# Gates of a hybrid block in pairs by seven half-size products, their weights split by accumulating DMA

## The chip, the cores and the metric

One core of a Trainium2 chip runs the kernel. The metric is the device time of one execution in microseconds; the kernel before is told by the median of three runs.

## The reference

One transformer block on 512 tokens of 1024 features, all in fp32. A normed input goes through one wide projection, four branches (attention, spatial gating, a short convolution, a multi-scale pool) give 256 features each, and each branch is widened to 1024 and gated:

```python
h = rmsnorm(x, norm_mix_pre[l])
(..., gate_pre) = split_cols(h @ w_in[l])
gates = jax.nn.sigmoid(gate_pre + gate_b[l]).reshape(B_, S_, N_BRANCH, D_)
...
merged = (gates[:, :, 0] * y_a + gates[:, :, 1] * y_b
          + gates[:, :, 2] * y_c + gates[:, :, 3] * y_d)
x = x + rmsnorm(merged @ w_out[l], norm_mix_post[l])
h = rmsnorm(x, norm_ffn_pre[l])
f = jnp.square(jax.nn.relu(h @ w_ff1[l])) @ w_ff2[l]
x = x + rmsnorm(f, norm_ffn_post[l])
```

`gate_pre` is 512 tokens by 4 x 1024: as a product, 32 output blocks of 128 features by 512 tokens, each over 1024 inputs.

## The kernel before, in words

Each fp32 product is three products of a shorter format. A matrix is held as a high part (a cast) and a low part (matrix minus cast), and `mm3` issues high x high, high x low and low x high. So every weight has to be split: `load` (line 110) has SP fetch 512 KB into one of three `raw` buffers; `split_w` (line 115) casts on ACT (`wh`) and subtracts on DVE (`wl`); `split_by_dma` (line 122) casts on ACT, writes the negated high part by ACT and lets a DMA issued by POOL add the weights from memory to it. Before, only the four early blocks of `w1` are split the second way. `wh` and `wl` have five buffers each, PSUM has eight banks.

**Order.** PE issues in the order of the program text. ACT, DVE, POOL and SP issue each in an order that a scheduler sets when the kernel is built; a waiting instruction holds back all that stands behind it on its engine. All instructions of PE and ACT are issued by a helper and are recorded at line 95, so they are told apart by tile.

**Gate stage.** `z` is the normed input, `zh` and `zl` its two parts, features on partitions, 512 tokens on columns. For each of eight blocks of 128 output features the loop at line 683 calls `gate(b, i)` for the four branches: 24 matmuls of 512 columns into a bank `fb` (line 329), then a product with the row scales `rbc` (line 452). `merge(b)` (line 457) takes sigmoids of the four gates, widens the branches by 24 matmuls with `wB[b]` into banks `y`, multiplies (line 468), adds (line 470), and splits the merged block into `mh` and `ml`. The gates of block 0 stand between the steps of the attention.

**Then** the product with `wO` (`wo`), a norm, and the feed-forward layer. `ff1` (line 718) gives the first four blocks of the hidden layer (`EARLY`, line 761) into banks `z`, first for 256 tokens, then for the other 256. The other blocks of `w1` go in pairs by seven half-size products (line 855): with the weights of a pair cut into four quarters and the input into four, sums of quarters are formed (`raw` combined by DVE; `hsum` of the input), and seven products `pa`, `pb`, `pc`, `pa` again, `pd`, `pc` again, `pa` again of 12 matmuls on 256 columns replace eight. `second()` (line 807) does one block of the second layer, `w2`, into the banks `acc`, with `uh` and `ul`, the two parts of the hidden block.

Of the kernel before, what the change touches and what calls it, by code (L numbers as in the profile page):

```python
# [80 lines left out]
def build(ctx, tc, d, out):  # L81
# [22 lines left out]
    def f(t):  # L104
        return t.bitcast(F32)
# [36 lines left out]
    def sl(pair, *ix):  # L142
        return pair[0][ix], pair[1][ix]
# [305 lines left out]
    def gate(b, i):  # L449
        ps = feature_block("wG", 4 * b + i)  # L450
        g = gp.tile([P, S], F32, tag="g", name="g", bufs=6)
        DVE.tensor_tensor(g, ps, rbc, ALU.mult)  # L452
        return g

    gates = []

    def merge(b):
        for i, g in enumerate(gates):
            ACT.activation(g, g, AF.Sigmoid, bias=k1("gateb")[:, i * 8 + b:i * 8 + b + 1])
        w = weights(d["wB"][b])  # L460
        prev = None
        for i, br in ((1, bT), (2, cT), (3, dT), (0, aT)):
            g = gates[i]
# [12 lines left out]
    others = branches()  # L476

# [188 lines left out]
    right = dict(side="right")  # L666

    TOP = 20
    xp = ctx.enter_context(tc.tile_pool(name="xp", bufs=1, reuse_waits="tile", **right))
    x1 = xp.tile([P, NT, D], F32, name="x1")  # L670
    r2 = xp.tile([P, TOP], F32, name="r2")[:, :NT]
    mp = ctx.enter_context(ExitStack())
    mpool = mp.enter_context(tc.tile_pool(name="mp", bufs=1, reuse_waits="tile", **right))
    mh = mpool.tile([P, KD, S], F32R, name="mh")
    ml = mpool.tile([P, KD, S], F32R, name="ml")
    mT = (mh, ml)
    gmix = mpool.tile([P, D], F32, name="gmix")
    gffn = mpool.tile([P, D], F32, name="gffn")
    for b in range(KD):
        while len(gates) < 4:  # L680
            gates.append(gate(b, len(gates)))
        merge(b)
    nc.sync.dma_start(gmix, d["gmix"].partition_broadcast(P))
    nc.sync.dma_start(gffn, d["gffn"].partition_broadcast(P))
    for t in range(NT):
        nc.sync.dma_start(x1[:, t, :], d["x"][t * P:(t + 1) * P, :])
    s1.close()

    HK, HS = KD // 2, S // 2
    hs = ExitStack()
    hp_ = hs.enter_context(tc.tile_pool(name="hp", bufs=1, reuse_waits="tile"))

# [4 lines left out]
    hsum = [hp_.tile([P, 3, HK, HS], F32R, name=f"hs{c}") for c in "hl"]  # L704
    ws = ExitStack()
    wk_ = ws.enter_context(tc.tile_pool(name="wk", bufs=1, reuse_waits="tile"))
    yg = wk_.tile([P, NT, D], F32, name="yg")
    stt = wk_.tile([P, NT, 4], F32, name="stt")

# [31 lines left out]
    for hf in range(2):  # L741
        wo = [weights(d["wO"][hf, c]) for c in range(4)]
        for t in range(NT):
            ps = bank("wo")
            for k in range(KD):
                mm3(ps, sl(mT, slice(None), k, slice(t * P, (t + 1) * P)),
                    sl(wo[k // 2], slice(None), slice((k % 2) * 512, (k % 2 + 1) * 512)), k == 0, k == KD - 1)
            cols = slice(hf * 512, (hf + 1) * 512)
            sq = wk_.tile([P, D], F32, tag="sq", name="sq", bufs=1)
            ACT.activation(sq[:, :512], ps, AF.Square, accum_out=stt[:, t, hf:hf + 1])  # L750
            DVE.tensor_tensor(yg[:, t, cols], ps, gmix[:, cols], ALU.mult)
            if hf == 0:
# [35 lines left out]
    sst = up.tile([P, 64], F32, name="sst")[:, :4 * NT].rearrange("p (t c) -> p t c", c=4)  # L788
# [50 lines left out]
    A11, A12, A22, S4 = (sl(h2, slice(None), k, t) for k, t in  # L839
                         ((slice(0, HK), slice(0, HS)), (slice(HK, KD), slice(0, HS)), (slice(HK, KD), slice(HS, S)),  # L840
                          (slice(0, HK), slice(HS, S))))
    S1, S2, S3 = (sl(hsum, slice(None), c) for c in range(3))
    fx = hs.enter_context(tc.tile_pool(name="fx", bufs=1, reuse_waits="tile"))
    B1, B2 = slice(0, 512), slice(512, 1024)

    def small():
        return fx.tile([P, HS], F32, tag="x", name="x", bufs=5)

    def part(ps, w, at, a, first):

        for k in range(HK):
            mm3(ps[:, :HS], sl(w, slice(None), slice(at + k * P, at + (k + 1) * P)), sl(a, slice(None), k),
                first and k == 0, k == HK - 1, not first)

    for j in range(EARLY, NFF, 2):
        g, h = u[j], u[j + 1]
        left, rght = load(d["w1"][j]), load(d["w1"][j + 1])
        w = split_w(left)
        w22 = split_w(rght[:, B2], 512)

        DVE.tensor_tensor(left[:, B1], rght[:, B1], left[:, B1], ALU.subtract)
        DVE.tensor_tensor(rght[:, B1], rght[:, B2], rght[:, B1], ALU.subtract)
        DVE.tensor_tensor(rght[:, B2], rght[:, B2], left[:, B1], ALU.subtract)
        DVE.tensor_tensor(left[:, B2], left[:, B2], rght[:, B2], ALU.subtract)
        wl = split_w(left)
        wr = split_w(rght)
        pa, pb = bank("pa"), bank("pb")
        part(pa, w, 0, A11, True)
        x1_ = small()
        ACT.copy(x1_, pa[:, :HS])  # L870
        part(pb, w, 512, A12, True)
        DVE.tensor_tensor(g[:, :HS], pb[:, :HS], x1_, ALU.add)
        if j == EARLY:
            second()
        pc = bank("pc")
        part(pc, wl, 0, S1, True)
        x5 = small()
        ACT.copy(x5, pc[:, :HS])
        part(pa, wr, 512, S2, False)
        x2 = small()  # L880
        ACT.copy(x2, pa[:, :HS])
        pd = bank("pd")
        part(pd, wl, 512, A22, True)
        second()
        part(pc, w22, 0, S4, False)
        DVE.tensor_tensor(h[:, :HS], pc[:, :HS], x2, ALU.add)
        part(pa, wr, 0, S3, False)
        x3 = small()
        ACT.copy(x3, pa[:, :HS])
        DVE.tensor_tensor(g[:, HS:], pd[:, :HS], x3, ALU.add)  # L890
        DVE.tensor_tensor(h[:, HS:], x3, x5, ALU.add)
# [131 lines left out]
```

## Time and profile before

| what | us |
|---|---|
| median of 3 runs (743.75 to 744.67) | 744.11 |
| the profiled execution | 744.92 |
| its span in the trace | 743.2 |
| PE busy | 728.5 |
| DVE busy | 467.2 |
| ACT busy | 356.5 |
| POOL busy | 15.9 |

The profiled execution's own time is its span and what lies around it. Busy times of engines overlap; a matmul's record is longer than the distance to the next (0.39 us against 0.227 for 512 columns), so the time of a group of matmuls is read from the chain, where consecutive ones are joined. Idle time of an engine counts only where another waits for it. The mean granted TensorE clock over the span is 1.00 of its upper level of 2.4 GHz.

### The profile page before, as it was taken

Reading aid. Unit: us, or ns where it says so; the run is one execution under the profiler, and the core shown is the slowest. Engines: PE = TensorE matmul, PEld = TensorE weight load, DVE = VectorE, ACT = ScalarE, POOL = GpSimd, SP = SyncE. Lnnn points to the kernel's source line nnn. Section 1 sums busy time; section 2 is a strip of 40 time slices with the busy share of each in tenths; the row PEclk is TensorE's granted clock in tenths of the full one; section 3 lists DMA queues with packets and bytes.
Section 4 is the critical chain, followed back from the end, with each engine's and each line's share of the span. In section 5 each row is a group of like instructions: output and inputs, shape, how many; then the busy total and the mean of one; then the engine's idle time right before and its main releaser. Section 6 shows DMA issues by size and latency. Waiting matters only on the chain.

```text
span 743.2 us, 10315 instructions
## 1 busy us (share of the span) xinstructions
PE 728.5 (98%) x4058; PEld 636.4 (86%) x4058; DVE 467.2 (63%) x760; ACT 356.5 (48%) x584; POOL 15.9 (2%) x32
## 2 busy tenths in 40 slices
PE   8999999999999999999997999999999999999996
PEld 8998788888888888888887899999999999888885
DVE  7599986355456365365355976777677676774424
ACT  6875444523323232332346756546665556753411
POOL 1110000000000000000011000000000000000001
PEclk9999999999999999999999999999999999999999
DMA  8523222362232322323137033322433233533103
GB/s 304 183 107 114 86 95 73 117 219 94 90 109 86 112 86 90 109 86 111 44 101 198 1 108 120 101 99 86 130 97 114 86 101 127 170 113 112 60 0 114
DMA packets 23728, 80.87 MB, mean 109 GB/s; under 512 B 3072, under 2 KB 3584, under 8 KB 23680
## 3 DMA queue, kind: packets, MB, share of 16 engines
q1 hardware_dynamic: 23072, 78.12, 31.2%
q0 software_dynamic: 608, 2.10, 1.6%
q8 instruction: 32, 0.52, 0.3%
q14 instruction: 16, 0.13, 0.1%
HBM read 78.11 MB, written 2.10 MB: 108 GB/s over the span
## 4 chain that ended last, share of the span: by engine, by line
PE 88%; DVE 5%; DMA 2%; ACT 2%; issue 1%; SPq 0%; POOL 0%; DVEq 0%; ACTq 0%; POOLq 0%
PE fb L95 28%; PE acc L95 23%; PE pa L95 8%; PE y L95 6%; PE wo L95 5%; PE pc L95 5%; PE pd L95 3%; PE pb L95 2%; PE psA L95 2%; PE sgv L95 2%; DMA xT<-in_xT 1%; PE po L95 1%; DMA wl<-in_w 1%; DMA raw<-in_wF 1%; DVE wl L119 1%
## 5 line engine op out<-in xcount | busy, mean ns | idle before, releaser
L95 ACT CAST wh<-raw 128x1024 fp32r<-128x1024 f32 (+2 forms) x154 | 153.7, 1009 | 222.3 <-issue 105.4
L119 DVE TENSOR_TENSOR wl<-raw,wh 128x1024 fp32r<-128x1024 f32 (+2 forms) x150 | 173.8, 1167 | 28.8 <-ACT wh L95 26.5
L95 PE MATMUL fb<-zh,wh 128*128 128x512 f32 x336 | 131.4, 391 | 0.1
L95 PE MATMUL fb<-zl,wh 128*128 128x512 f32 x336 | 130.8, 389 | 0.0
L95 PE MATMUL fb<-zh,wl 128*128 128x512 f32 x336 | 130.8, 389 | 0.0
L95 PE MATMUL acc<-wh,ul 128*128 128x512 f32 x232 | 90.5, 390 | 1.2 <-DVE ul L798 1.2
L95 PE MATMUL acc<-wh,uh 128*128 128x512 f32 x232 | 90.7, 391 | 0.0
L95 PE MATMUL acc<-wl,uh 128*128 128x512 f32 x232 | 90.6, 391 | 0.0
L452 DVE TENSOR_TENSOR g<-fb,rbc 128x512 f32<-128x512 f32 x32 | 22.1, 692 | 96.7 <-PE fb L95 96.7
L798 DVE TENSOR_TENSOR ul<-u,uh 128x512 fp32r<-128x512 f32 x58 | 38.7, 689 | 57.2 <-ACT uh L95 57.1
L95 PEld LDWEIGHTS fb<-zh,wl 128*128 128x128 f32 x336 | 63.1, 188 | 13.2
L95 PEld LDWEIGHTS fb<-zh,wh 128*128 128x128 f32 x336 | 63.1, 188 | 13.2 <-DVE zc L361 0.4
L95 PEld LDWEIGHTS fb<-zl,wh 128*128 128x128 f32 x336 | 63.1, 188 | 12.8
L95 PEld LDWEIGHTS acc<-wh,ul 128*128 128x128 f32 x232 | 43.6, 188 | 11.4 <-DVE ul L798 2.1
L95 PEld LDWEIGHTS acc<-wh,uh 128*128 128x128 f32 x232 | 43.6, 188 | 8.5 <-ACT uh L95 0.4
L95 ACT CAST uh<-u 128x512 fp32r<-128x512 f32 x58 | 34.3, 618 | 34.2 <-PE acc L95 33.7
L95 PEld LDWEIGHTS acc<-wl,uh 128*128 128x128 f32 x232 | 43.6, 188 | 7.9
L95 ACT ACTIVATE u<-u 128x512 f32<-128x512 f32 x60 | 33.2, 622 | 16.3 <-DVE u L890 16.3
L95 PE MATMUL pa<-hsh,wh 128*128 128x256 f32 x112 | 31.3, 280 | 0.5 <-ACT x L95 0.5
L95 PE MATMUL pa<-hsl,wh 128*128 128x256 f32 x112 | 31.2, 279 | 0.0
L95 PE MATMUL pa<-hsh,wl 128*128 128x256 f32 x112 | 31.2, 279 | 0.0
L95 PE MATMUL wo<-wh,mh 128*128 128x512 f32 x64 | 25.1, 392 | 0.0
(313 smaller groups left out, 1419.7 us busy)
## 6 DMA issues: line engine op xcount, KB each, us to landing
raw<-in_w SPq DMA_DIRECT2D x64, 512.0 KB, 3.5
raw<-in_wG SPq DMA_DIRECT2D x32, 512.0 KB, 3.4
raw<-in_wF SPq DMA_DIRECT2D x10, 512.0 KB, 4.1
raw<-in_wB SPq DMA_DIRECT2D x8, 512.0 KB, 3.4
raw<-in_wO SPq DMA_DIRECT2D x8, 512.0 KB, 3.4
xk<-in_x SPq DMA_DIRECT2D x4, 512.0 KB, 9.3
x<-in_x SPq DMA_DIRECT2D x4, 512.0 KB, 5.8
wl<-in_w POOLq DMA_DIRECT2D x4, 512.0 KB, 6.5
```

The lines of the kernel that those rows point to most:

```text
L95: ins = op(*a, **k)
L119: DVE.tensor_tensor(lo[:, :n], raw[:, :n], f(hi)[:, :n], ALU.subtract)
L452: DVE.tensor_tensor(g, ps, rbc, ALU.mult)
L798: DVE.tensor_tensor(ul, u[j], f(uh), ALU.subtract)
```

## The change

The gates of blocks 2 to 7 are computed two at a time by the seven products that the feed-forward loop had already (`seven`, a generator that yields after each product, and `forms`, the quarters of the input). For it, sums of quarters of `z` are formed during block 1 (`z_sums`). In each pair of gates, the low parts of the first weight block and of the last quarter come by `split_by_dma`; the two combined blocks are split by ACT and DVE. `wB[b]` has tiles of its own, `bh` and `bl`, always split by DMA, and asked for a block ahead. The four groups of `y` of a block stand between the products of the next block's first pair. The merged block has a tile for each b. The loads of `x`, `gmix` and `gffn` come after those of `wO`. In the early feed-forward part, `ff1` issues the 16 products with the high weights first and then the 8 with the low ones, and the first `second()` moves behind `pa` and `pb` of the first pair.

```diff
-    def split_by_dma(src):
-
-        raw = load(src)
-        hi = wp.tile([P, 1024], F32R, tag="wh", name="wh", bufs=5)
-        lo = wp.tile([P, 1024], F32R, tag="wl", name="wl", bufs=5)
-        ACT.copy(hi, raw)
-        ACT.activation(lo, f(hi), AF.Copy, scale=-1.0)
-        POOL.dma_start(lo, src.bitcast(F32R), accum_op=ALU.add)
+    def split_by_dma(src, raw=None, n=1024, own=None):
+
+        raw = load(src, n) if raw is None else raw
+        if own is None:
+            hi = wp.tile([P, 1024], F32R, tag="wh", name="wh", bufs=5)
+            lo = wp.tile([P, 1024], F32R, tag="wl", name="wl", bufs=5)
+        else:
+            hi, lo = [own.tile([P, 1024], F32R, tag=f"b{c}", name=f"b{c}", bufs=1) for c in "hl"]
+        ACT.copy(hi[:, :n], raw[:, :n])
+        ACT.activation(lo[:, :n], f(hi)[:, :n], AF.Copy, scale=-1.0)
+        POOL.dma_start(lo[:, :n], src.bitcast(F32R), accum_op=ALU.add)
         return hi, lo
...
+    def seven(srcs, forms, small, g, h, by_dma):
+
+        A11, A12, A22, S1, S2, S3, S4 = forms
+        left, rght = load(srcs[0]), load(srcs[1])
+        if by_dma:
+            w = split_by_dma(srcs[0], left)
+            w22 = split_by_dma(srcs[1][:, B2], rght[:, B2], 512)
+        else:
+            w = split_w(left)
+            w22 = split_w(rght[:, B2], 512)
+
+        DVE.tensor_tensor(left[:, B1], rght[:, B1], left[:, B1], ALU.subtract)
...
+        wl = split_w(left)
+        wr = split_w(rght)
+        pa, pb = bank("pa"), bank("pb")
+        part(pa, w, 0, A11, True)
+        x1 = small()
+        ACT.copy(x1, pa[:, :HS])
+        yield
+        part(pb, w, 512, A12, True)
+        DVE.tensor_tensor(g[:, :HS], pb[:, :HS], x1, ALU.add)
+        yield
...
+        part(pc, wl, 0, S1, True)
...
+        part(pa, wr, 512, S2, False)
...
+        part(pd, wl, 512, A22, True)
...
+        part(pc, w22, 0, S4, False)
...
+        part(pa, wr, 0, S3, False)
...
-    def merge(b):
-        for i, g in enumerate(gates):
+    def merge(b, w):
+
+        gs = list(gates)
+        gates.clear()
+        for i, g in enumerate(gs):
             ACT.activation(g, g, AF.Sigmoid, bias=k1("gateb")[:, i * 8 + b:i * 8 + b + 1])
-        w = weights(d["wB"][b])
...
+            yield
-        ACT.copy(mh[:, b, :], prev)
-        DVE.tensor_tensor(ml[:, b, :], prev, f(mh)[:, b, :], ALU.subtract)
-        gates.clear()
+        ACT.copy(mT[0][b], prev)
+        DVE.tensor_tensor(mT[1][b], prev, f(mT[0][b]), ALU.subtract)
...
+    steps = merge(0, split_by_dma(d["wB"][0], own=wbp))
+    for i in range(4):
+        next(steps)
+    rest(steps)
+    for i in range(4):
+        gates.append(gate(1, i))
+        if i % 2 == 0:
+            z_sums(i // 2)
...
+    w = split_by_dma(d["wB"][1], own=wbp)
+    for b in range(2, KD):
+        steps = merge(b - 1, w)
+        for i in (0, 2):
+            g, h = (gp.tile([P, S], F32, tag="g", name="g", bufs=6) for _ in range(2))
+            for n, _ in enumerate(seven((d["wG"][4 * b + i], d["wG"][4 * b + i + 1]), ops, small_g, g, h, True)):
+                if i == 0 and n in (1, 2, 4, 5):
+                    next(steps)
+                if i == 0 and n == 5:
+                    rest(steps)
+                    w = split_by_dma(d["wB"][b], own=wbp)
+            for x in (g, h):
+                DVE.tensor_tensor(x, x, rbc, ALU.mult)
+            gates.extend((g, h))
+    rest(merge(KD - 1, w))
...
     def ff1(j, w, ps, lo, hi):
-        for k in range(KD):
-            mm3(ps[:, lo:hi], sl(w, slice(None), slice(k * P, (k + 1) * P)), sl(h2, slice(None), k, slice(lo, hi)),
-                k == 0, k == KD - 1)
+
+        for c, parts in ((0, (0, 1)), (1, (0,))):
+            for k in range(KD):
+                for p in parts:
+                    PE.matmul(ps[:, lo:hi], w[c][:, k * P:(k + 1) * P], h2[p][:, k, lo:hi],
+                              start=c == 0 and k == 0 and p == 0, stop=c == 1 and k == KD - 1)
...
-        if j == EARLY - 1:
-            second()
         pend.append((j, usplit(j)))
...
     for j in range(EARLY, NFF, 2):
         g, h = u[j], u[j + 1]
...
+        for n, _ in enumerate(seven((d["w1"][j], d["w1"][j + 1]), ops, small, g, h, False)):
+            if n == 4 or n in (1, 2) and j == EARLY:
+                second()
```

**ACT in a block of the gate stage.** Before, a stretch from the end of one merge on (`wh` casts of gate and branch weights, `g` sigmoids, `mh` the merged block):

```order
L95 CAST wh_2734<-raw_2732 128x1024
L95 CAST mh_1650<-g_2448 128x512
L95 CAST wh_2777<-raw_2775 128x1024
L95 ACTIVATE g_2627<-g_2627,c1_109 128x512
L95 CAST wh_2810<-raw_2808 128x1024
L95 ACTIVATE g_2660<-g_2660,c1_109 128x512
```

Now, in the first pair of a block (`raw_3311` and `raw_3313` are the second pair's combined blocks, `raw_3284` is `wB`, `raw_3441` the next block's first pair, `x` the results of parts):

```order
L95 CAST wh_3329<-raw_3311 128x1024
L95 CAST wh_3333<-raw_3313 128x1024
L95 CAST bh_3286<-raw_3284 128x1024
L95 ACTIVATE bl_3287<-bh_3286 128x1024
L95 COPY x_3303<-pa_3159 128x256
L95 CAST wh_3445<-raw_3441 128x1024
L95 CAST mh5_1886<-g_3002 128x512
L95 COPY x_3351<-pa_3337 128x256
L95 ACTIVATE wl_3446<-wh_3445 128x1024
L95 CAST wh_3450<-raw_3443 128x512
```

A cast, now and then a sigmoid, became a run of casts and negated copies; between the cast of the next block's first weights and its negated copy stand the merged block's cast and an `x` copy.

**POOL around the gate stage.** Before:

```order
L433 MEMSET zc_982 128x2
L433 MEMSET zc_1217 128x2
L129 DMA wl_3339<-in_w1 128x1024
L147 TENSOR_TENSOR stt_2975<-stt_2975,nhalf_71 128x1 x3
L129 DMA wl_3371<-in_w1 128x1024
```

Now:

```order
L505 MEMSET zc_1217 128x2
L132 DMA bl_1669<-in_wB 128x1024
L132 DMA wl_1906<-in_wG 128x1024
L132 DMA bl_1895<-in_wB 128x1024
L132 DMA wl_1911<-in_wG 128x512
L132 DMA wl_2084<-in_wG 128x1024
L132 DMA wl_2089<-in_wG 128x512
L132 DMA bl_2055<-in_wB 128x1024
L132 DMA wl_2214<-in_wG 128x1024
```

Where POOL issued nothing, it now issues five accumulating DMAs a block, 32 more in all, in one queue.

**DVE in the early feed-forward part.** Before, from the first `ul` on (`u30`, `u31` hold sums for a later product, `hl` its low part, `raw_3690` and `raw_3692` are the first pair of `w1`; the weights of the first `acc` had been split 18 instructions ahead):

```order
L798 TENSOR_TENSOR ul_3602<-u1_3529,uh_3601 128x512
L837 TENSOR_TENSOR hl_2968<-u30_3500,hh_2967 128x2x256
L798 TENSOR_TENSOR ul_3632<-u2_3528,uh_3631 128x512
L861 TENSOR_TENSOR raw_3690<-raw_3692,raw_3690 128x512
L837 TENSOR_TENSOR hl_2968<-u31_3499,hh_2967 128x2x256
```

Now (`wl_4533` and `wl_4537` are of the pair, `wl_4572` is of the first `acc`):

```order
L940 TENSOR_TENSOR ul_4446<-u1_4373,uh_4445 128x512
L977 TENSOR_TENSOR hl_3803<-u30_4344,hh_3802 128x2x256
L940 TENSOR_TENSOR ul_4476<-u2_4372,uh_4475 128x512
L351 TENSOR_TENSOR raw_4516<-raw_4516,raw_4518 128x512
L977 TENSOR_TENSOR hl_3803<-u31_4343,hh_3802 128x2x256
L360 TENSOR_TENSOR u4_4370<-pb_4541,x_4554 128x256
L119 TENSOR_TENSOR wl_4533<-raw_4516,wh_4532 128x1024
L119 TENSOR_TENSOR wl_4537<-raw_4518,wh_4536 128x1024
L119 TENSOR_TENSOR wl_4572<-raw_4569,wh_4571 128x1024
```

The split of the first `acc` weights moved from ahead of the `ul` to behind them and behind the pair's own two splits.

## Rows read from the trace of the kernel before

**Rows 1.** The page: busy time by engine, and the chain that ended last.

```profile
PE 728.5 (98%) x4058; PEld 636.4 (86%) x4058; DVE 467.2 (63%) x760; ACT 356.5 (48%) x584; POOL 15.9 (2%) x32
...
PE 88%; DVE 5%; DMA 2%; ACT 2%; issue 1%; SPq 0%; POOL 0%; DVEq 0%; ACTq 0%; POOLq 0%
```

**Rows 2.** Chain of waits, 157 to 348 us: start us, us, what.

```profile
157.32 21.76 PE fb L95 x96
179.08 5.44 PE y L95 x24
```

**Rows 3.** Chain of waits, 340 to 486 us: early and steady feed-forward.

```profile
398.24 5.55 DMA wl<-in_w
...
427.20 1.40 PE pb L95 x12
...
475.35 1.40 PE pa L95 x12
```

**Rows 4.** Windows: stretch, length, PE, PEld, DVE, ACT, POOL busy us, PEclk, DMA share, GB/s.

```profile
157.00:348.00 191.00, 191.00 (x844) 158.16 (x843) 99.04 (x121) 59.16 (x71) 0.00 (x0) 1.00 0.31 104
...
396.00:402.00 6.00, 3.52 (x30) 3.31 (x29) 3.96 (x10) 4.98 (x8) 2.28 (x3) 1.00 0.95 249
...
460.00:490.00 30.00, 30.00 (x215) 28.14 (x214) 21.22 (x29) 17.99 (x30) 0.00 (x0) 1.00 0.33 100
...
740.00:743.20 3.20, 0.00 (x0) 0.00 (x0) 0.00 (x0) 0.00 (x0) 0.00 (x0) 0.50 0.44 164
```

**Rows 5.** Groups by form, DVE: count, then busy us, mean ns, idle before.

```profile
L119 DVE TENSOR_TENSOR wl<-raw,wh 128x1024 fp32r<-128x1024 f32 x134 | 162.7, 1223 | 28.3 <-ACT wh L95 26.0 <-issue 0.3
...
L452 DVE TENSOR_TENSOR g<-fb,rbc 128x512 f32<-128x512 f32 x32 | 22.1, 692 | 96.7 <-PE fb L95 96.7
...
L863 DVE TENSOR_TENSOR raw<-raw 128x512 f32<-128x512 f32 x14 | 9.7, 692 | 0.5
...
L872 DVE TENSOR_TENSOR u<-pb,x 128x256 f32<-128x256 f32 x14 | 5.9, 418 | 0.0
```

**Rows 6.** Groups by form, ACT: the same columns.

```profile
L95 ACT CAST wh<-raw 128x1024 fp32r<-128x1024 f32 x138 | 143.7, 1052 | 210.3 <-issue 105.4 <-PE pc L95 45.4 <-PE fb L95 39.6
...
L95 ACT ACTIVATE g<-g,c 128x512 f32<-128x512 f32 x32 | 23.0, 719 | 0.0
...
L95 ACT COPY x<-pa 128x256 f32<-128x256 f32 x42 | 15.4, 367 | 3.8 <-PE pa L95 2.5
...
L95 ACT CAST wh<-raw 128x512 fp32r<-128x512 f32 x15 | 9.3, 622 | 12.1 <-PE pd L95 10.9 <-DMA raw<-in_w 1.1
...
L95 ACT ACTIVATE wl<-wh 128x1024 fp32r<-128x1024 f32 x4 | 4.3, 1065 | 0.1
```

**Rows 7.** Tile wl on POOL, the accumulating DMAs: issue to landing, last line.

```profile
DMA to landing us min/median/max: 5.6/6.5/7.6
```

**Rows 8.** The page's DMA queues and issues; last, DMA issues of 391 to 406 us.

```profile
q1 hardware_dynamic: 23072, 78.12, 31.2%
...
q0 software_dynamic: 608, 2.10, 1.6%
...
raw<-in_wG SPq DMA_DIRECT2D x32, 512.0 KB, 3.4
...
raw<-in_w SPq DMA_DIRECT2D x3, 512.0 KB, 7.1
```

**Rows 9.** Timeline of ACT, then PE, around the first merge: start us, us, what.

```profile
145.46 1.05 ACT L95 CAST wh<-raw 128x1024 fp32r<-128x1024 f32 x1 [2.55 <-PE fb L95]
...
152.13 0.39 PE L95 MATMUL y<-bh,wl 128*128 128x512 f32 x1
```

**Rows 10.** PE's waits (us, times, longest); DVE's timeline in the early feed-forward part.

```profile
PE z L95 <- DMA wl<-in_w: 3.7, 2, 2.5
...
PE acc L95 <- DVE ul L798: 1.2, 1, 1.2
...
422.50 1.29 DVE L798 TENSOR_TENSOR ul<-u,uh 128x512 fp32r<-128x512 f32 x2
```

More of the change, by code (lines that the diff above doesn't have):

```diff
@@ L455, in build @@
     gates = []
-    def merge(b):
-        for i, g in enumerate(gates):
+    def merge(b, w):
+        gs = list(gates)
+        gates.clear()
+        for i, g in enumerate(gs):
             ACT.activation(g, g, AF.Sigmoid, bias=k1("gateb")[:, i * 8 + b:i * 8 + b + 1])
-        w = weights(d["wB"][b])
         prev = None
-        for i, br in ((1, bT), (2, cT), (3, dT), (0, aT)):
-            g = gates[i]
+        for i, br in ((1, bT), (2, cT), (3, dT), (0, aT)) if b == 0 else enumerate((aT, bT, cT, dT)):
+            g = gs[i]
             ps = bank("y")
@@ L668, in build @@
     TOP = 20
-    xp = ctx.enter_context(tc.tile_pool(name="xp", bufs=1, reuse_waits="tile", **right))
-    x1 = xp.tile([P, NT, D], F32, name="x1")
[L671 to L696, printed above, removed]
+    mp = ctx.enter_context(ExitStack())
+    mT = [], []
+    def merged(name, pad):
+        pool = mp.enter_context(tc.tile_pool(name=name, bufs=1, reuse_waits="tile", **right))
+        for b in range(HK):
+            for c in range(2):
+                mT[c].append(pool.tile([P, S], F32R, name=f"m{'hl'[c]}{len(mT[c])}"))
+        if pad:
+            pool.tile([P, TOP], F32, name="top")
@@ new lines, in build, with small_g, rest @@
+    merged("mp0", True)
+    s4 = ExitStack()
+    wbp = s4.enter_context(tc.tile_pool(name="wbp", bufs=1, reuse_waits="tile"))
+    ss = s4.enter_context(tc.tile_pool(name="ss", bufs=1, reuse_waits="tile"))
+    ss.tile([P, 8], F32, name="shift")
+    zsum = [ss.tile([P, 3, HK, HS], F32R, name=f"zs{c}") for c in "hl"]
+    def small_g():
+        return ss.tile([P, HS], F32, tag="x", name="x", bufs=5)
+    def rest(steps):
+        for _ in steps:
+            pass
+    while len(gates) < 4:
+        gates.append(gate(0, len(gates)))
@@ new lines, in build, with z_sums @@
+    tq = ExitStack()
+    tqp = tq.enter_context(tc.tile_pool(name="tq", bufs=1, reuse_waits="tile", **right))
+    lower = []
+    def z_sums(hh):
+        q = tqp.tile([P, 4, 2, HS], F32, name=f"q{hh}")
+        a11, a12, a21, a22 = (q[:, c] for c in range(4))
+        for c, (k, t) in enumerate(((0, 0), (HK, 0), (0, HS), (HK, HS))):
+            ix = slice(None), slice(k + 2 * hh, k + 2 * hh + 2), slice(t, t + HS)
+            DVE.tensor_tensor(q[:, c], f(zh)[ix], f(zl)[ix], ALU.add)
+        DVE.tensor_tensor(a22, a21, a22, ALU.add)
+        DVE.tensor_tensor(a21, a11, a21, ALU.subtract)
+        DVE.tensor_tensor(a11, a22, a11, ALU.subtract)
+        DVE.tensor_tensor(a12, a12, a11, ALU.subtract)
+        for c, v in enumerate((a22, a11, a21)):
+            ix = slice(None), c, slice(2 * hh, 2 * hh + 2)
+            ACT.copy(zsum[0][ix], v)
+            DVE.tensor_tensor(zsum[1][ix], v, f(zsum[0])[ix], ALU.subtract)
+        lower.append(a12)
@@ new lines, in build @@
+    steps = merge(0, split_by_dma(d["wB"][0], own=wbp))
[6 more added lines that the diff above has]
+            z_sums(i // 2)
+    for hh, v in enumerate(lower):
+        ix = slice(None), slice(2 * hh, 2 * hh + 2), slice(HS, S)
+        ACT.copy(zh[ix], v)
+        DVE.tensor_tensor(zl[ix], v, f(zh)[ix], ALU.subtract)
+    tq.close()
+    merged("mp1", False)
+    ops = forms(z, zsum)
+    w = split_by_dma(d["wB"][1], own=wbp)
@@ L697, in build @@
+    rest(merge(KD - 1, w))
+    s4.close()
+    s1.close()
+    xp = ctx.enter_context(tc.tile_pool(name="xp", bufs=1, reuse_waits="tile"))
+    x1 = xp.tile([P, NT, D], F32, name="x1")
+    r2 = xp.tile([P, lines(NT)], F32, name="r2")[:, :NT]
     hs = ExitStack()
@@ L706, in build @@
     wk_ = ws.enter_context(tc.tile_pool(name="wk", bufs=1, reuse_waits="tile"))
+    gmix = wk_.tile([P, D], F32, name="gmix")
+    gffn = wk_.tile([P, D], F32, name="gffn")
+    nc.sync.dma_start(gmix, d["gmix"].partition_broadcast(P))
+    nc.sync.dma_start(gffn, d["gffn"].partition_broadcast(P))
+    for t in range(NT):
+        nc.sync.dma_start(x1[:, t, :], d["x"][t * P:(t + 1) * P, :])
     yg = wk_.tile([P, NT, D], F32, name="yg")
@@ L745, in build @@
             for k in range(KD):
-                mm3(ps, sl(mT, slice(None), k, slice(t * P, (t + 1) * P)),
+                mm3(ps, sl([m[k] for m in mT], slice(None), slice(t * P, (t + 1) * P)),
                     sl(wo[k // 2], slice(None), slice((k % 2) * 512, (k % 2 + 1) * 512)), k == 0, k == KD - 1)
@@ L847, in small @@
         return fx.tile([P, HS], F32, tag="x", name="x", bufs=5)
[L849 to L853, printed above, removed]
+    ops = forms(h2, hsum)
     for j in range(EARLY, NFF, 2):
         g, h = u[j], u[j + 1]
[L857 to L891, printed above, removed]
```

36 lines of the change are left out of this document (30 added, 6 removed).

## Prediction

> **What bounds the kernel now.** I read the page's busy shares first: TensorE (PE) is at work for 728.5 of 743.2 us, and 88% of the chain that ended last is PE [rows 1]. So a change pays only by what it takes off PE's own list, and it costs wherever PE then waits. The chain of waits through the gate stage shows the pattern there: four gate products of 24 matmuls in 21.76 us, one group of 24 `y` matmuls in 5.44 us, and again, with nothing in between [rows 2]; seven such blocks of 27.2 us stand in it after the first merge. The windows say what is free beside it: from 157 to 348 us PE is busy for 191.00 of 191.00 us, VectorE (DVE) for 99.04, ScalarE (ACT) for 59.16, at a DMA share of 0.31 [rows 4]. So PE alone sets that stage, and DVE, ACT and the DMA engines have room that the change will spend. The feed-forward loop already works with seven half-size products: one part of 12 matmuls on 256 columns takes 1.40 us [rows 3], and there from 460 to 490 us PE is busy for all 30.00 us, DVE for 21.22 and ACT for 17.99 [rows 4].
>
> **What PE saves.** A pair of gate products costs 2 x 5.44 = 10.88 us (21.76 / 4 each, [rows 2]). Seven parts cost 7 x 1.40 = 9.80 us [rows 3]. That is 1.08 us a pair; blocks 2 to 7 have 12 pairs: **-13.0 us**. A block comes to 19.60 + 5.44 = 25.04 us where it was 27.2. The matmuls' kinds are those of rows that exist, so this term is the surest.
>
> **What the others pay, per block.** DVE, by the means of its groups [rows 5]: for a pair four combinations of 0.69, two low parts of 1.22, four operations of 0.42 and two products with `rbc` of 0.69 us, 8.3 in all; two pairs and the merge (four products, three sums and one low part, each like the product with `rbc`: 5.5) make 22.0 of 25.04 us. ACT [rows 6]: for a pair three casts of 1.05, a negated copy of 1.07, a half-width cast and copy of 0.62 each and four `x` copies of 0.37, 6.9 in all; two pairs, the branches' cast and negated copy, four sigmoids of 0.72 and the half-width cast of the merged block make 19.5. DMA: five plain loads and four units of 512 KB by the accumulating queue. The page's queues give 31.2% of the span for 78.12 MB and 1.6% for 2.10 MB, or 1.56 and 2.97 us of all 16 engines per 512 KB [rows 8]: 5 x 1.56 + 4 x 2.97 = 19.7 of 25 us. All three fit beside PE, at 88, 78 and 79%. None sets the period by its sum; what can set it is a chain of them, so I followed the chains.
>
> **The steady block.** Count from the first matmul of a block's first pair; in the new orders ACT runs, after the casts for `wl` and `wr`: `bh`, `bl`, an `x` copy, the next pair's `wh`, `mh`, another `x` copy, and that pair's `wl` copy, after which POOL may issue. With durations of [rows 6]: the combination of the second pair's halves lets its `wr` be cast at 12.5; `bh` ends at 14.9, `bl` at 15.9, `x` at 16.2, `wh` at 17.2 (its raw block, asked for at 12.1, needs 3.4 us [rows 8] and, with a microsecond for its neighbours, is there by 16.6), `wl` at 18.95. POOL issues at 19.25. What follows is the price I know least: the four accumulating DMAs of before landed 5.6, 6.5 (median) and 7.6 us after the issue [rows 7]. So the low part lands between 24.85 and 26.85, and PE's third matmul of the next block wants it at 25.27. That is a wait of 0 to 1.6, and to 2.0 if the transfer also shares the engines with `bl`. At the median it is 0.5; `bl`'s own accumulate is under way when it starts, so I take 0.9. Five times: **+4.5 us, from 0 to +10**. The other low parts have over a microsecond to spare: the second pair's `w` lands by 14.5 and is wanted at 15.5, and `bl` has the rest of its block.
>
> **A page's figure for the same transfer.** The Trainium skill, "DMA: Bandwidth & Descriptors", section on the anatomy of one DMA, fits a GpSimd transfer as about 2.0 us plus its bytes over 436e3 per us: an estimate of 3.2 us for 512 KB. By it no steady block would wait, the first merge would wait 0.5, and the sum would be 7.8 us lower. The rows say 5.6 to 7.6 [rows 7] and decide here.
>
> **The first merge.** Block 0's branch weights were split by a DVE subtraction; now their low part comes by DMA. ACT casts the next gate's weights at 145.46 [rows 9], then `bh`, a sigmoid, and `bl` by 149.1 (1.05 + 0.72 + 1.07); POOL issues at 149.4 and the low part lands at 155.0 to 157.0. PE's third `y` matmul ran at 152.13 [rows 9]. A wait of 2.9 to 4.9, at the median **+3.8 us**; nothing stands behind it that PE could do, its order being written.
>
> **The early feed-forward part.** Its high-weight matmuls now go first, so the two waits for low parts, 3.7 us [rows 10], are mostly covered; I take back 1.5, since the chain of DVE and ACT work behind them started only at the end of `wo`. Against that, `acc` moves behind `pa` and `pb`, and its weights are now cast behind the pair's. Before, DVE was through with the `ul` by 423.8 [rows 10], and the first `acc` group, `pa` and `pb` had run by 428.60 (427.20 + 1.40, [rows 3]). Now DVE still does after `ul` two `hl`, one `ul` and one combination (4 x 0.6), an `u` (0.4) and three splits (3 x 1.14, spaced by ACT's casts), which gives 429.5 at the old times, some 427.8 with what the covered waits bring forward. `acc` then ends at 430.55, 1.95 later; two smaller waits of 0.15 and 0.5 of the old order go. **+1.3 us**, from -3.7 (both old waits vanish and nothing is late) to +2.9 (nothing is brought forward).
>
> **At nothing:** the sums of `z` (DVE and ACT work during block 1, where both had half of the time free [rows 4]; without that cover some 16 us of DVE would stand in the path); the last merge, whose `mh` is due 4.8 us after the last `y` and by the durations above ready after 4.0; the loads of `x`, `gmix` and `gffn`, now behind those of `wO`, whose readers have eight banks of `wo` products ahead of them.
>
> **Sum.** -13.0 + 3.8 + 4.5 + 1.3 = -3.4. The profiled execution took 744.92 us (span 743.2), 0.81 above the median 744.11. So 741.5 for such an execution and **740.7** for the median. Lower ends: -13.0 + 2.9 + 0 - 3.7 = -13.8; upper ends: -13.0 + 4.9 + 10 + 2.9 = +4.8.
>
> **Rivals.**
> (a) Full cover. The accumulates land in 5.6 to 6 us and the early part gains. For it: the one issued at 398.24 landed in 5.55 us [rows 3], most of them at a DMA share of 0.95 [rows 4]. Against it: that leaves 0.4 us to spare in a chain of eight steps. -13.8: 730.3. Chance 0.17.
> (b) Slower: the raw block of the next pair comes late, because SP's loads share the engines with the accumulates. For it: while three accumulates ran, from 391 to 406 us, SP's loads took 7.1 us instead of 3.4 [rows 8]. Against it: there three accumulates and three loads met within 10 us, here four units and five loads are spread over 25. With 7.1 the block lands at 19.2, is cast by 20.25, copied by 21.3, issued at 21.6, and its low part lands at 28.1, 2.8 late: 5 x 2.8 = 14.0 in place of 4.5, +6.1, 750.2. It decides from 1.6 us per block on, (13.0 - 3.8 - 1.3) / 5, that is from a landing at 26.9. Chance 0.22.
> (c) No change: waits of 1.2 to 1.9 us a block, the upper part of my own term, 742.6 to 745.6. A measurement of this kernel tells changes from 0.2%, 1.5 us, on. Chance 0.10.
> (d) The clock. The granted clock stood at 1.00 through a wait of 2.5 us [rows 4, 10] and fell to 0.50, the 1.2 GHz level, in the last stretch, after PE's last matmul [rows 4]. My waits of 3.8 and some 5 us lie between these. If it fell in them, what follows runs at half speed: between nothing and a whole merge and one `acc` group twice over, 5.44 + 2.75; half of that is +4, 744.7. Chance 0.05. The Trainium skill, "TensorE: Matmul & The Clock Gate", Part 1, has such a rule: an idle gap drops the engine to the lower clock. By that rule the two long gaps would be dearer than their length; the trace agrees as far as its end goes, and shows no such fall in the middle.
> (e) The splits cannot keep pace: DVE at 88% has no row like it; its highest share in a PE-bound stretch is 21.22 of 30, 71% [rows 4]. What its order makes wait I count inside (b) and (c).
>
> **How the numbers follow.** My forecast has 0.46, with 0 to 1.1 us of wait per block and the early part at -0.5 to +2 its own range is 734.5 to 742.5; with (a), 0.17, faster is 0.63. (c) and (d) make same 0.15, (b) makes slower 0.22. The range runs from 731 to 749, where (a) and (b) each keep about a tenth outside.
>
> **What would show it.** In the profile after: twelve times seven gate parts of 1.40 us; PE `y` waiting once for DMA `bl`, about 3.8; PE `pa` waiting five times for DMA `wl` of the gates, 0 to 2 each; PE `acc` waiting about 5 for DVE or ACT in place of 1.2, and `z` less than 3.7; POOL with 36 accumulates; in the gate stage DVE near 85%, DMA share near 0.75, clock 1.00. I am wrong if the parts take over 1.45 us, if landings leave 5.6 to 7.6, or if PE waits there for DVE or ACT splits.

## The result, and the profile after

The changed kernel takes 753.27 us (median of 4 runs, 750.91 to 754.81) beside 744.07 us of the kernel before: a ratio of 1.012, 95% interval 1.0092 to 1.0147. It is slower, where 740.7 and faster was forecast, and lies outside the range of 731 to 749. The profiled execution is the fastest of the four, 750.91 us, span 749.2; what follows explains its 6.0 us over the span before of 743.2. The other three were not traced.

The page after, busy time and chain, for [rows 1]:

```profile
PE 723.5 (97%) x4490; PEld 650.4 (87%) x4490; DVE 518.3 (69%) x872; ACT 418.6 (56%) x696; POOL 43.5 (6%) x64
...
PE 70%; DVE 10%; DMA 8%; issue 7%; ACT 3%; POOL 1%; SPq 0%; DVEq 0%; POOLq 0%; ACTq 0%
```

PE has 5 us less to do by its busy time, and still ends later: its share of the chain went from 88 to 70%, and the rest is now chains of other engines and of DMAs. PE's waits, for [rows 10] (total, times, longest):

```profile
PE pa L95 <- DMA wl<-in_wG: 6.1, 5, 1.8
PE acc L95 <- ACT wh L95: 3.6, 1, 3.6
PE y L95 <- DMA bl<-in_wB: 3.0, 1, 3.0
PE z L95 <- DMA wl<-in_w: 2.2, 2, 1.5
PE acc L95 <- DVE wl L119: 1.1, 1, 1.1
```

Before, the waits for `z`, for `ul` and for one `x` copy made 5.4 us in all; the waits for the gates' low parts, for `bl` and for the first `acc` weights are new. The windows, for [rows 4], behind three of these waits, and the blocks 2 to 7 (columns as there, the granted clock is the third from the end):

```profile
156.00:158.00 2.00, 2.00 (x6) 1.56 (x5) 1.35 (x3) 0.00 (x0) 0.00 (x0) 0.50 1.07 193
319.00:321.00 2.00, 2.00 (x11) 2.00 (x11) 0.25 (x1) 1.85 (x4) 0.00 (x0) 0.50 0.87 274
432.00:434.00 2.00, 2.00 (x6) 1.53 (x5) 0.64 (x1) 1.05 (x1) 0.00 (x0) 0.50 0.95 360
183.00:344.00 161.00, 154.88 (x1147) 147.61 (x1146) 120.28 (x186) 103.25 (x157) 24.15 (x28) 0.99 0.72 171
```

Behind the waits the granted clock stood at 0.50, its 1.2 GHz level; in the kernel before it did so nowhere ahead of the last matmul. Over the blocks DVE is busy for 120.28 of 161 us and the DMA share is 0.72, 0.31 before. The chain of waits, for [rows 2, 3], at the first merge and in the blocks:

```profile
148.01 5.91 DMA bl<-in_wB
...
153.97 6.87 PE y L95 x22
160.84 21.76 PE fb L95 x96
182.60 1.43 PE pa L95 x12
184.03 1.44 PE pb L95 x12
185.47 1.39 PE y L95 x6
186.86 1.40 PE pc L95 x12
...
229.41 6.84 DMA wl<-in_wG
...
283.07 6.83 DMA wl<-in_wG
...
309.76 7.67 DMA wl<-in_wG
...
319.12 2.56 PE pb L95 x12
```

A part of the products takes 1.43 or 1.44 us where the moving operand is `z`, and 1.40 to 1.42 where it is a sum of `z` (the `pc` at 186.86); six `y` matmuls take 1.39, a quarter of [rows 2]'s 5.44 is 1.36. In the first merge PE spends 6.87 us on 22 matmuls, some of them at the lower clock, and at 319.12 a part takes 2.56, all of it at the lower clock. The landings of the accumulating DMAs, for [rows 7], first of `bl`, then of `wl`:

```profile
DMA to landing us min/median/max: 5.9/7.3/9.2
```

```profile
DMA to landing us min/median/max: 3.8/6.0/8.1
```

Where the 6.0 us lie, from the starts of the same matmuls in both timelines:

| stretch | before, us | after, us | difference | forecast |
|---|---|---|---|---|
| start to the first `y` | 151.57 | 150.24 | -1.3 | 0 |
| first merge | 5.59 | 10.44 | +4.9 | +3.8 |
| block 1 to the first `wo` | 190.40 | 189.13 | -1.3 | -13.0 + 4.5 |
| `wo` to part `pb` of the third feed-forward pair | 113.73 | 117.46 | +3.7 | +1.3 |
| the rest | 281.9 | 281.9 | 0.0 | 0 |

### The profile page after: what moved, and what is told of

Read it like the earlier page. It is cut to its first block, busy times and chain, and to the rows that moved or that the text cites. A ratio compares the mean times of both kernels' runs of the same rounds, so it can differ in the third digit from the quotient of the medians.

```text
span 749.2 us, 11527 instructions
## 1 busy us (share of the span) xinstructions
PE 723.5 (97%) x4490; PEld 650.4 (87%) x4490; DVE 518.3 (69%) x872; ACT 418.6 (56%) x696; POOL 43.5 (6%) x64
## 4 chain that ended last, share of the span: by engine, by line
PE 70%; DVE 10%; DMA 8%; issue 7%; ACT 3%; POOL 1%; SPq 0%; DVEq 0%; POOLq 0%; ACTq 0%
PE acc L95 24%; PE pa L95 11%; PE fb L95 8%; PE pc L95 8%; PE wo L95 5%; PE pb L95 4%; PE y L95 4%; PE pd L95 4%; DMA wl<-in_wG 3%; DVE wl L119 2%; DMA xk<-in_x 1%; DMA raw<-in_wO 1%; DMA xT<-in_xT 1%; PE po L95 1%; DMA bl<-in_wB 1%
## 5 line engine op out<-in xcount | busy, mean ns | idle before, releaser
L95 ACT CAST wh<-raw 128x1024 fp32r<-128x1024 f32 (+2 forms) x170 | 164.6, 980 | 132.2 <-PE pc L95 61.0
L119 DVE TENSOR_TENSOR wl<-raw,wh 128x1024 fp32r<-128x1024 f32 (+2 forms) x142 | 163.9, 1164 | 44.0 <-ACT wh L95 41.8
L95 PE MATMUL fb<-zh,wh 128*128 128x512 f32 x144 | 56.7, 394 | 0.1
L95 PE MATMUL fb<-zh,wl 128*128 128x512 f32 x144 | 56.1, 390 | 0.0
L95 PE MATMUL fb<-zl,wh 128*128 128x512 f32 x144 | 56.1, 390 | 0.0
L95 ACT COPY x<-pa 128x256 f32<-128x256 f32 x78 | 28.6, 367 | 25.7 <-PE pa L95 24.2
L95 PEld LDWEIGHTS fb<-zh,wl 128*128 128x128 f32 x144 | 27.0, 188 | 5.8
L95 PEld LDWEIGHTS fb<-zh,wh 128*128 128x128 f32 x144 | 27.1, 188 | 5.7 <-DVE zc L433 0.4
L95 PEld LDWEIGHTS fb<-zl,wh 128*128 128x128 f32 x144 | 27.1, 188 | 5.2
L542 DVE TENSOR_TENSOR g<-g,y 128x512 f32<-128x512 f32 x32 | 21.7, 682 | 10.2 <-PE y L95 10.2
```

Source lines behind the costliest of these rows:

```text
L95: ins = op(*a, **k)
```

## Experiments

Theory A: a wait of PE in this kernel costs its length and then a stretch of matmuls at half clock, and three such places, with parts of 1.43 us, used up the gain. The rivals stand with each run, and `e1` to `e4` are edits of the changed kernel. Each ratio is to the kernel before, run on the same chip.

**The first merge by DVE.** `e1`, beside the changed kernel:

```diff
-    steps = merge(0, split_by_dma(d["wB"][0], own=wbp))
+    raw0 = load(d["wB"][0])
+    w0 = [wbp.tile([P, 1024], F32R, tag=f"b{c}", name=f"b{c}", bufs=1) for c in "hl"]
+    ACT.copy(w0[0], raw0)
+    DVE.tensor_tensor(w0[1], raw0, f(w0[0]), ALU.subtract)
+    steps = merge(0, w0)
```

> The changed kernel, with the low part of block 0's branch weights subtracted by DVE instead of added by a DMA. Theory A (a wait of PE costs its length and then a stretch at half clock): the first merge takes 10.4 us in the profile of the change against 5.5 before, of which 3.0 is the wait and about 2 the half clock behind it; here both go, 5 us less than the changed kernel, about 748. Rival B (the clock falls for another reason, such as the load on the other engines): only the 3.0 of the wait go, and the granted clock still shows a stretch at 0.50 near 156 us. Rival C (DVE is late there, behind the sums of z): no gain.

Measured: 745.06 us, ratio 0.9998 (0.9983 to 1.0012). The first merge takes 5.59 us. The window behind it, and what is left of PE's waits:

```profile
156.00:158.00 2.00, 2.00 (x10) 1.66 (x9) 1.97 (x5) 1.74 (x2) 0.00 (x0) 1.00 0.85 156
```

```profile
PE pa L95 <- DMA wl<-in_wG: 4.4, 5, 1.2
PE acc L95 <- ACT wh L95: 3.7, 1, 3.7
```

The clock is at 1.00 in the same place as soon as the wait is gone, so Rival B falls, and with a merge of 5.59 us Rival C too: it is the wait that brings the clock down. The median lies 8.2 us under that of the changed kernel, more than the 5 forecast; of the spans it is 749.2 to 743.1, 6.1, since the blocks, which this edit leaves alone, were shorter too: the gates' waits came to 4.4 in place of 6.1, and no fall followed the last of them.

**The second layer's first group early again.** `e2`:

```diff
         ACT.activation(u[j], u[j], AF.Square)
+        if j == EARLY - 1:
+            second()
         pend.append((j, usplit(j)))
...
-            if n == 4 or n in (1, 2) and j == EARLY:
+            if n == 4 or n == 1 and j == EARLY:
```

> The changed kernel, with the first group of acc put back ahead of pa and pb, in the place it had before; the order of the high and low products in the early part stays changed. Theory A: the 3.6 and 1.1 us of waits for the split of the first acc weights and the half clock behind them, together 4.6 by the two traces, go; some 1 us of wait for ul returns: 3.5 to 4.5 us less than the changed kernel, about 749. Rival B: the waits go, 3.5 at most, and the clock falls elsewhere. Rival C (the chain of DVE and ACT work before acc is as late as ever, so PE waits the same time earlier): within 1 us of the changed kernel.

Measured: 745.42, ratio 1.0005 (0.9991 to 1.0018). From `wo` to the third pair it needs 113.09 us, 4.4 less than the changed kernel's 117.46 and 0.6 less than before; the median lies 7.9 us under it.

```profile
PE y L95 <- DMA bl<-in_wB: 3.8, 1, 3.8
...
PE acc L95 <- DVE ul L940: 1.2, 1, 1.2
```

Theory A holds for the size in this stretch, Rivals B and C fall: 1.2 us of wait for `ul` stands where 4.7 stood. The wait in the first merge came to 3.8 here, and behind it the granted clock is again down, 0.64 from 156 to 158 us and 0.51 from 158 to 160.

**The first pair's low part by DVE.** `e3`:

```diff
-            w = split_by_dma(srcs[0], left)
+            w = split_by_dma(srcs[0], left) if w_dma else split_w(left)
...
-            for n, _ in enumerate(seven((d["wG"][4 * b + i], d["wG"][4 * b + i + 1]), ops, small_g, g, h, True)):
+            for n, _ in enumerate(seven((d["wG"][4 * b + i], d["wG"][4 * b + i + 1]), ops, small_g, g, h, True, not (i == 0))):
```

> The changed kernel, with the low part of the first weight block of each block's first pair subtracted by DVE; the second pair and the branch weights stay with the DMA. Theory A: the five waits of PE for that low part (6.1 us in the profile of the change) go, and the half clock behind them (1.3 us there, more in the slower runs): 6 to 9 us less than the changed kernel, 744 to 747, and the blocks come to 25.5 us each. Rival D (DVE has no room for it: 1.2 us more on 22 of 25): PE waits for DVE splits instead, less than 3 us gained. Rival E (another chain, raw loads or the other accumulates, is as late): waits for wl of the second pair or for bl appear, less than 3 us gained.

Measured: 745.88, ratio 1.0014 (1.0005 to 1.0024). The waits for `wl` of the gates are gone, none for another low part came up, and one of 0.8 us for an `x` copy remains. Windows:

```profile
156.00:158.00 2.00, 2.00 (x6) 1.54 (x6) 0.27 (x1) 0.00 (x0) 0.00 (x0) 0.50 0.04 8
426.00:428.00 2.00, 2.00 (x6) 1.52 (x6) 0.51 (x1) 1.04 (x1) 0.00 (x0) 0.50 0.96 338
185.00:338.00 153.00, 152.20 (x1145) 145.83 (x1145) 125.08 (x190) 100.19 (x152) 19.80 (x23) 1.00 0.68 162
```

The third row is the blocks: PE busy for 152.20 of 153 us with DVE at 125.08. So Rivals D and E fall, and a block comes to 25.7 us. From block 1 to the first `wo` it is 181.3 us, 7.8 less than in the changed kernel. The first two rows show the lower clock behind the two waits that were left in (4.2 us for `bl`, 3.7 for the `acc` weights).

**All three.** `e4` has the three edits.

> All three edits together. Theory A: the gains add, 14 to 18 us less than the changed kernel, 735 to 739, and no stretch at half clock between the start and the last matmul; the seven parts stay at 1.43 us where their moving operand is z. Rivals: less by what the single runs show, or less than their sum if one wait hides behind another.

Measured: 735.27, ratio 0.9873 (0.9856 to 0.9889), in the range expected and 1.3% faster than the kernel before. The gains do not simply add: the three single medians lie 8.2, 7.9 and 7.4 us under the changed kernel, 23.5 in all, and this one 18.0. The traces show a part that is counted more than once: from block 1 to the first `wo`, `e1` and `e2` need 185.9 and 186.3 us where the changed kernel needs 189.1, with shorter waits for low parts of the gates that neither edit touches. And one point missed: the clock did fall once ahead of the end.

```profile
PE z L95 <- DMA wl<-in_w: 2.1, 1, 2.1
```

```profile
390.00:392.00 2.00, 0.18 (x1) 0.18 (x2) 0.70 (x3) 2.00 (x4) 0.40 (x2) 1.00 0.98 229
392.00:394.00 2.00, 2.00 (x11) 2.00 (x12) 1.23 (x1) 0.38 (x1) 0.59 (x1) 0.54 1.05 199
394.00:396.00 2.00, 2.00 (x13) 2.00 (x12) 0.00 (x0) 0.00 (x0) 0.00 (x0) 0.60 1.04 190
```

The first window, nearly all wait, is still at 1.00, and the two behind it are at 0.54 and 0.60.

**The place of `z`.** `e5` is `e4` with `z` and the branch tiles, which are the moving operands of the gates and of `y`, 32 bytes further on:

```diff
+    zp.tile([P, 8], F32, name="shiftz")
     zh = zp.tile([P, KD, S], F32R, name="zh")
...
     aT, bT, cT, dT = halves("a"), halves("b"), halves("c"), halves("d")
+    outs.tile([P, 8], F32, name="backz")
```

> The kernel with all three edits, and z and the branch tiles 32 bytes further on in each partition, where the sums of z and the feed-forward input already lie (all of those at 32 in 64 bytes, z at 0). Theory F (the parts whose moving operand is z are slow for where z lies): their distance falls from 0.120 to 0.117 us a matmul, y from 0.232 to 0.227, a block from 25.7 to 25.2, in all 2 to 3 us less than that kernel. Rival G (they are slow for what the other engines and DMAs do meanwhile): no change beyond 0.5 us, the distance stays at 0.120.

Measured: 735.58, ratio 0.9885 (0.9872 to 0.9897), no different from `e4`. The chain, block 1's gates, then a part on `z`, a `y` group and a part on the sums:

```profile
157.00 22.40 PE fb L95 x96
179.40 1.40 PE pa L95 x12
...
182.20 1.40 PE y L95 x6
183.61 1.44 PE pc L95 x12
```

Theory F is half right: the parts on `z` fall to 1.40 in part of the cases. But the 96 matmuls of block 1 rise from 21.76 to 22.40, `y` stays, though its operand moved, and the parts on sums, not moved, rise from 1.40 to 1.44. So moving tiles changes the durations, but the place of the moving operand alone does not tell which way; the cause, and what would be best, stays open.

**The first early `w1` block by DVE.** `e6` is `e4` with

```diff
-        w, ps = split_by_dma(d["w1"][j]), bank("z")
+        w, ps = (split_by_dma if j else weights)(d["w1"][j]), bank("z")
```

> The kernel with all three edits, and the low part of the first of the four early w1 blocks subtracted by DVE, so that three accumulates run there instead of four. The trace of the three edits has one wait of 2.1 us for such a low part at 390 us, with a granted clock of 0.54 and 0.60 in the 4 us behind it. Theory A: that wait goes, and the half clock with it: 3 to 4 us less. Rival: the accumulate of the next block is as late, and nothing is gained.

Measured: 733.53, ratio 0.9859 (0.9846 to 0.9872), 1.7 us under `e4`, which ran on another chip; by the ratios it is 0.14%, 1.0 us, with intervals that overlap. In its trace no stretch of 2 us from 140 to 470 us is under 0.97 in granted clock.

```profile
PE z L95 <- DMA wl<-in_w: 2.2, 2, 1.5
...
PE acc L95 <- DVE ul L944: 1.1, 1, 1.1
```

The sum of the waits is as before, in two pieces of at most 1.5. The gain is less than the 3 to 4 us expected and can hardly be told from nothing: the fall went, the wait stayed.

**The old order of the early products.** `e7` is `e4` with `mm3` over the eight slices in `ff1` as before.

> The kernel with all three edits, and the early part's products in the order of before (high, high, low for each of eight slices instead of all 16 with the high weights first). This prices the term of the prediction that gave the new order 1.5 us. If it holds, PE waits 1.5 us or more longer for the low parts of w1 (3.7 in all before) and, by theory A, the clock falls there: 1.5 to 4 us slower than the three edits. Rival: the wait of 2.1 is there in either order and the order is worth nothing.

Measured: 735.40 (733.98 to 738.40), ratio 0.9889 (0.987 to 0.9908): in the middle as fast as `e4`, with more than twice its spread. In the profiled run, 737.63, one of the slower:

```profile
PE z L95 <- DMA wl<-in_w: 3.5, 1, 3.5
```

and the clock is at 0.50 from 390 to 396 us. So the new order does shorten the wait, by 1.4 us here, and the gain in the median can't be told from nothing.

**Shift and DVE split.** `e8` has the edits of `e5` and `e6`.

> The three edits with the shift of z and the DVE split of the first early w1 block. If both theories hold, 5 to 7 us less than the three edits, 728 to 731; if neither, no change.

Measured: 735.99, ratio 0.9895 (0.9877 to 0.9913). The 5 to 7 us expected if both theories held did not come: the kernel is no faster than `e4` or `e5`.

**No accumulating DMA in the gate stage.** `e10` is `e6` with `seven(..., False)` for the gates and `wB` split by `ACT.copy` and a DVE subtraction into `bh` and `bl`.

> The kernel with the three edits and the first early w1 block split by DVE (the best so far, 733.5), with every low part of the gate stage, also those of the branch weights, subtracted by DVE: no accumulating DMA there. By the working of the prediction DVE then has 27.0 us of work a block (22.0, two splits of 1.22, two of 0.69 and one of 1.22) against PE's 25.5, so DVE sets the block: 27 to 28 us, 9 to 14 us slower, 743 to 748, with waits of PE for DVE splits. Rival: since DVE's instructions follow each other closer than their mean durations, it still fits and nothing changes. For the distance of the matmuls on z: if it is the accumulating DMAs that make it 0.120, it falls to 0.117 here; if not, it stays.

Measured: 738.29, ratio 0.9923 (0.9903 to 0.9943), 4.8 us more than `e6`, half of the least that was expected, and still under the kernel before. PE's waits, and the window over the blocks:

```profile
PE pa L95 <- DVE wl L119: 3.3, 5, 0.8
```

```profile
181.00:331.00 150.00, 146.68 (x1091) 139.51 (x1090) 138.00 (x208) 79.12 (x124) 0.00 (x0) 1.00 0.30 96
```

DVE is busy for 138 of 150 us, 92%, and PE waits for its splits. But a block comes to 26.3 us where 27 to 28 was expected, so DVE does not yet set it: its instructions start closer together than their mean durations (behind a split of 1.22 us the next one starts 1.14 after it), and those of this window add to 151 us by duration. The parts on `z` stay at 1.43 and 1.44 us, 0.120 a matmul, without an accumulating DMA beside them: the accumulating DMAs are not what makes them slow.

**The products undone.** `e11` is `e6` with `gate(b, i)` for the four gates of a block, one group of `y` behind each, and no sums of `z`.

> The best so far, with the gates of blocks 2 to 7 as four products of 24 matmuls again and no sums of z; the y groups still stand between the gates, the branch weights still come by DMA into tiles of their own a block ahead. It prices the seven products by themselves: six blocks of 27.2 us against 25.6 there. Theory: 9 to 10 us slower, 742.5 to 744, hence all of the gain over the kernel before comes from the products and none from the rest. Rival: the new order and tiles are worth something, or cost something, and it comes out 2 us or more from that.

Measured: 779.54, ratio 1.0474 (1.0444 to 1.0503), far off, for a reason of its own:

```profile
PE y L95 <- DMA bl<-in_wB: 25.8, 6, 10.2
```

With the last group of `y` behind the last gate, the next `bl` is asked for one gate, 5.4 us, before it is wanted. It prices no product. Its six waits do bear on Theory A: behind those of 3.0, 4.0, 3.0 and 10.2 us the clock fell, behind those of 2.7 and 2.9 it did not. Windows behind the fourth (2.97) and the fifth (2.92):

```profile
310.00:312.00 2.00, 2.00 (x6) 1.63 (x5) 0.69 (x1) 0.00 (x0) 0.00 (x0) 0.50 0.23 94
342.00:344.00 2.00, 2.00 (x10) 1.68 (x9) 0.69 (x1) 0.00 (x0) 0.00 (x0) 1.00 0.21 86
```

`e13` puts two groups of `y` behind each of the first two gates (against `e11`):

```diff
             new.append(gate(b, i))
-            next(steps)
-            if i == 3:
+            if i < 2:
+                next(steps), next(steps)
+            if i == 1:
                 rest(steps)
                 w = split_by_dma(d["wB"][b], own=wbp)
```

> As the run with the products undone, but with the y groups behind the first two gates of a block, so that the next block's branch weights are asked for two gates earlier (there PE waited 25.8 us for them, which hid the price of the products). Against the three edits with the first early w1 block by DVE (733.5): if the seven products are worth what the blocks show, 27.2 against 25.6 us, 9 to 10 us slower, 742.5 to 744, the time of the kernel before; then all of the gain comes from them. Rival: the rest of the change is worth or costs 2 us or more, and it comes out that far from 743.

Measured: 743.15, ratio 0.9978 (0.9968 to 0.9988), as expected. Against `e6`, 0.9859, the products are worth 1.2%, some 9 us; all the rest, once its waits are mended, 0.2%. The traces agree: from block 1 to the first `wo` this kernel needs 190.40 us, as before, and `e6` 180.77, 9.6 less.

**Two early blocks by DVE.** `e12` is `e6` with `j > 1` in place of `j`.

> The best so far, with the low parts of the first two early w1 blocks subtracted by DVE. Its trace still has two waits for such low parts, 2.2 us in all and 1.5 the longest. If DVE has room at the end of the wo stage, 1 to 2 us less, 732; if its splits hold up the norm behind wo, nothing or a little slower.

Measured: 732.99, ratio 0.9844 (0.9825 to 0.9862), the fastest here; `e6` lies inside its interval.

## Why the prediction was wrong

**The step that failed** is the price of a wait. The prediction took each as its length, and put a fall of the clock into rival (d), with a chance of 0.05, because [rows 4, 10] show 1.00 through one wait of 2.5 us. That row was one case on the kind side. In the profiled runs here every wait of PE of 3.0 us or more (3.0, 3.8, 4.2 for `bl`, 3.0, 3.0, 4.0 and 10.2 for it in `e11`, 3.6, 3.7, 3.7 for the first `acc` weights, 3.5 for `z`) has matmuls at a granted clock near 0.50 behind it. Between 1.8 and 2.9 it went either way: one of 1.8 (the changed kernel) and one of 2.1 (`e4`) have too, while one of 1.8 (`e13`), that of 2.5 in the kernel before and those of 2.7 and 2.9 in `e11` have not; nor have those of up to 1.7. So in that stretch the length alone does not decide, and what does is not shown. After the first merge's wait of 3.0 us the merge took 10.44 where 5.59 is its length without: 1.9 more than the wait. That the wait is the cause and not the place is what `e1`, `e2` and `e3` show, each of which takes the wait at one place away and the fall with it; that it is not the accumulating DMA as such shows in `e2`, where none was taken away. The page of the Trainium skill that was cited there, "TensorE: Matmul & The Clock Gate", Part 1, was the better guide: an idle gap drops the clock. By it rival (d) should have been part of the forecast; the traces agree in that each fall ahead of the end stands behind a gap, though gaps of up to 2.9 us also passed without one.

**The saving** of -13.0 was a mis-sized term. Without waits six blocks take 153.5 us (`e6`, from the first `pa` to the last merge), 25.6 each, against 25.04 forecast: -9.7. The parts on `z` take 1.43 where [rows 3], of another operand in another place, gave 1.40, and `y` 1.39 for 1.36. `e13` prices the whole saving at some 9 us.

**The steady block** was the right chain with a wrong landing. POOL's issues in the blocks 2 to 4:

```profile
148.01 0.92 POOL L132 DMA_DIRECT2D bl<-in_wB  x1 [51.07 <-ACT bl L95]
...
201.91 0.85 POOL L132 DMA_DIRECT2D wl<-in_wG  x1 [2.10 <-ACT wl L95]
...
229.41 0.87 POOL L132 DMA_DIRECT2D wl<-in_wG  x1 [2.10 <-ACT wl L95]
...
256.50 0.86 POOL L132 DMA_DIRECT2D wl<-in_wG  x1 [2.98 <-ACT wl L95]
```

The second to fourth rows are issues for the next block's first pair, 19.5 us after the block's first part in the first block, as forecast (19.25), and 21 in the later ones, where the block's own wait has come in between. They landed after 6.8 to 7.7 us by the chain, not 6.5, and by `wl`'s rows up to 8.1: PE waited five times as predicted, and lost 6.9 us by the starts of its matmuls (6.1 in the list above, which begins a wait where a matmul's record ends) instead of 4.5. The last of the five drew a fall of the clock, 1.5 more. With the saving, -9.7 + 6.9 + 1.5 gives the -1.3 of the table. One sum of the prediction's chain does not come out of its own terms: from the end of `bh` to that of the `wl` copy the durations that it names add to 4.55 us, it wrote 4.05, and the trace has 4.05 (197.56 to 201.61), as ACT starts an instruction before the record of the one ahead has ended.

**The first merge** waited 3.0 us for `bl` (3.8 forecast; POOL issued at 148.01, 1.4 earlier than worked out, as the merge began 1.3 earlier, and it landed after 5.91), and paid 1.9 for the clock.

**The early part.** The chain that was to make `acc` late was named rightly:

```profile
424.64 0.50 DVE hl L977
...
426.48 1.05 ACT wh L95
...
428.70 2.37 DVE wl L119 x2
...
431.11 4.38 PE acc L95 x11
```

DVE ends the weights' split at 431.07. Counted from the first `wo`, 2.25 us later than before, that is 428.8 at the old times, between the 427.8 and 429.5 of the prediction (the terms listed there add to 430.0, not 429.5); PE's waits of 4.7 us are the 5 forecast. The clock behind them took 2 us more, and `z` gave back its 1.5 (2.2 us of wait left of 3.7). So +3.7 in place of +1.3.

**Left out:** the 1.3 us that the changed kernel is earlier at the first `y`. Some 0.6 lie ahead of the first branch products; the rest lies in the attention, where the order of DVE and ACT is another one. Neither was followed further.

**The rivals.** (b), slower, came true in the sign, but its mechanism did not: the raw loads of the gates landed after 3.7 us in the median, not 7.1. (d) was the mechanism and was priced at +4; the three falls of the profiled run come to 1.9 + 1.5 + 2, about 5. From the 741.5 forecast for a profiled execution the way goes by +3.3 of saving that was not there, +2.4 of waits in the blocks, -0.8 in the first merge, +5.4 of falls and -1.3 at the start to 750.5; 0.4 of the 750.91 are left in small pieces. That the other three runs took 2 to 4 us longer fits more falls (mean granted clocks of 0.989, 0.989 and 0.990 against 0.991); by an estimate from these means, 0.75 us lost for each 0.001 of 750 us, that is 0.8 to 1.5 us, and the rest is not shown. (e), DVE, did not bind in the gate stage: only in `e10`, with every split on it, PE waited for it there.

## What to carry to other kernels

Price a new wait of the matrix engine at its length and a stretch at half clock behind it, 1.5 to 2.5 us in the changed kernel and in `e3`: all waits of 3.0 us and more paid it, none of up to 1.7 did, and between them one row without a fall is no proof, as the 2.5 us of the kernel before showed. A change that trades work for such waits needs more than its count of matmuls. A step that fills the pipeline once (a first merge, a first group) may be better served by the short path, here a DVE subtraction of about a microsecond, than by the DMA that serves the steady state, and with the waits gone the saving of the steady state shows: 733.5 us in place of 744. When the same operation is to run on another operand, take its duration as a range: 0.1166 us a matmul became 0.120 for no cause that the rows show.

## What was not expected of the hardware

The granted clock fell to the lower level in the middle of a kernel whose PE is busy for 97% of the span, behind single waits of 1.8 to 4.2 us (10.2 in `e11`), and it did not behind others of up to 2.9. The distance between matmuls of 256 columns was 0.1166 to 0.120 us from one moving operand to another, and shifting `z` by 32 bytes made 512-column matmuls on it 3% slower (22.40 for 21.76 us) while it made some 256-column ones faster (1.40 for 1.43 a part). And the accumulating DMAs landed 3.8 to 9.2 us after their issue, those of half size among them. The estimate from the Trainium skill's "DMA: Bandwidth & Descriptors", section on the anatomy of one DMA, 3.2 us for 512 KB, is under all of them.
